# Two transformer blocks on one core: the norms' gains in rows, held weight splits, and a new order in the mixers

## The chip, the cores and the metric

The kernel runs on one core of a Trainium2 chip. The core has five engines that run their own instruction lists in order and meet at semaphores: TensorE (PE, matmuls into PSUM), VectorE (DVE), ScalarE (ACT), GpSimd (POOL) and SyncE (SP, which here issues most DMAs). The metric is the time of one execution in microseconds (us); lower is better.

## What is computed

256 tokens of width 1024 in float32 go through two blocks.

```
h = layer_norm(x, ln_in)                                   # block 1
for l in 0, 1:
    mix = mixer(h)      # MLA, differential and forgetting attention, one w_in, one w_out
    h   = layer_norm(alpha * h + mix, ln1[l])
    ffn = grouped_moe(h)   # router: 16 experts in 4 groups, top 2; silu(h wg) * (h wu) @ wd
    h   = layer_norm(alpha * h + ffn, ln2[l])
mem_k, mem_v = split(rms_norm(mem) @ mem_wkv)              # block 2
for i in 0, 1:
    x += 0.5 * swiglu(rms_norm(x), ffn1[i])
    x += ssd_pool_mixer(rms_norm(x)) if i == 0 else swa_sink_attention(rms_norm(x))
    x += memory_cross_attention(rms_norm(x), mem_k, mem_v)
    x += 0.5 * swiglu(rms_norm(x), ffn2[i])
```

The MLA part has 8 heads, the differential and the forgetting parts 4 each; the forgetting part adds cumulated log-sigmoid decays to its scores. The window attention has 16 heads, 4 key heads, a window of 128, a linear bias per head and one sink per head; the cross attention has 4 heads of width 256 over 256 memory rows.

## The kernel before

The tokens are two tiles of 128 rows (`t` = 0, 1). A product that must be exact to float32 is three matmuls on split numbers, `mm3` (L483 to L485): each operand is a high part `h` and a rest `l`, and hi·hi, hi·lo and lo·hi are summed in PSUM. `split` (L488, L489) makes the two from an activation: a copy on ScalarE, a subtraction on VectorE. The experts' and the memory's weights are used as plain float32 and aren't split.

All weights come through the class `Stream` (L66): a list of 1 MB transfers on SP's queue, into rings of 7 "stage" and 6 "piece" tiles, in the order of a plan (`plan`, L331). A weight to be split is read from its stage tile: a copy on ScalarE (L161) and a subtraction on VectorE (L162) into a piece tile. `hold(key)` stops these splits before a key, `go()` lets them run on. A raw expert tile is used where it lands, and may land in a buffer of the activations that is free (a slot: `m1`, `m4`, `xl`, `xh`). A framework's scheduler sets the order on each engine from the program's order, the dependences, and `with self.after(...)`, which puts instructions behind given ones.

Block 1's mixer (`mixer`, L818) takes w_in in six column blocks, runs MLA's heads between blocks 2 and 3, and the other two attentions behind the last. Its parts named below: the copies of the memory's keys on VectorE (L1729), the rotation tables (L744), the copies of MLA's values on ScalarE (L966), the softplus of the forget gates with its table load (L655, in `fox_decay`, L1071). A norm (`LayerNorm`, L194) is done tile by tile as the sums of a layer come in: `ln_norm` (L570) leaves out gain and bias, which are then applied in columns on the transposed rows (L548, L550, or at the experts' gather L1319, L1320, with the router's weights multiplied by them once) and later in rows (`gain`, L601 and L602); `ln_full` (L592 to L596) applies them at once with two passes over a tile.

The experts (`moe`, L1208) go in pairs, `pr` = 0 to 7: gate and up (L1352), transposes (L1369), down (L1386), and a scatter (L1401) whose results VectorE adds to the residual (L1403). Four gathers (L1317) fetch the tokens' columns. Memory products (L1758) fill TensorE beside the router and behind the last scatter.

In block 2 the SSD mixer's heads run four at a time (L2166, L2175) with the products for z (L1623 to L1625, copied out at L2189) in between; the window attention (`swa`) computes keys and values, both halves of the queries, and then the heads pair by pair: scores (L1980, L1982), bias and maximum (L2000), softmax, transposes and values; the cross attention (`xattn`) computes queries (L1831), scores and values between two products, `xq` and `xo`.

## Time and profile before

| | us |
|---|---|
| median of 3 runs | 2002.53 |
| lowest, highest | 2001.2, 2002.54 |
| profiled execution | 2002.3 |
| its span | 2000.5 |
| TensorE busy in the span | 1935.0 (97%) |
| VectorE, ScalarE busy | 1127.0, 866.9 |
| mean granted clock | 0.986 of full |

The page of a profile gives busy times, then the span in forty slices with the granted clock of TensorE in tenths. A view of waits sums, for each line, how long the engine stood idle just before it and which instruction released it. A timeline lists instructions by start; a bracket at the end of a row is the idle time before it and its releaser. A view of windows gives busy time, granted clock and the DMA engines' share for stretches of time.

### The profile page before, as it was taken

To read this page: it belongs to the slowest core of one execution; us is meant where nothing else is said; L and a number is where in the kernel's file an instruction comes from. 1 tells how busy PE (TensorE), PEld (TensorE's weight loads), DVE (VectorE), ACT (ScalarE), POOL (GpSimd) and SP (SyncE) were. 2 spreads that over 40 slices of the span, in tenths; PEclk is the share of its full clock that TensorE was granted. 3 is DMA by queue.
4 is the path that set the end of the run, shared out by engine and by line. 5 is a ranking of instruction groups with operands and counts; after the bars stand their busy time and mean duration, and the time that the engine had idled before them with its cause. 6 is when DMAs were issued, how large, how long until landed. Compare 5 with 4: busy or idle time off the path is not lost.

```text
span 2000.5 us, 28009 instructions
## 1 busy us (share of the span) xinstructions
PE 1935.0 (97%) x11069; PEld 1458.6 (73%) x11069; DVE 1127.0 (56%) x2211; ACT 866.9 (43%) x1539; POOL 58.0 (3%) x119
## 2 busy tenths in 40 slices
PE   6999999999999998899999899999999999999999
PEld 6776433367864333599988887899989986778998
DVE  7775122167751221656579775655665567766554
ACT  6563110136631101455466555644454455556443
POOL 1110000000100000000001000000000000000000
PEclk9999999999999999999999999999999997999999
DMA  8456999973569999855564353455555543335550
GB/s 290 145 203 229 397 419 420 421 256 123 206 236 403 420 421 421 300 187 181 186 202 137 132 219 109 163 190 190 190 200 186 182 165 137 127 99 175 190 190 22
DMA packets 176044, 453.39 MB, mean 227 GB/s; under 512 B 11120, under 2 KB 106844, under 8 KB 149148
## 3 DMA queue, kind: packets, MB, share of 16 engines
q1 hardware_dynamic: 172044, 435.55, 59.1%
q0 software_dynamic: 3856, 15.91, 2.2%
q8 instruction: 91, 1.49, 0.3%
q14 instruction: 53, 0.43, 0.1%
HBM read 446.19 MB, written 5.24 MB: 226 GB/s over the span
## 4 chain that ended last, share of the span: by engine, by line
PE 56%; DMA 5%; DVE 3%; ACT 2%; issue 0%; POOL 0%; DVEq 0%; SPq 0%; POOLq 0%; ACTq 0%
PE mm L1623 7%; PE mm L1625 7%; PE mm L1624 7%; PE accb L485 5%; PE accb L484 5%; PE accb L483 4%; PE acca L485 4%; PE acca L484 4%; PE acca L483 4%; DMA piece<-in_exp_w_gate_dram 2%; DMA piece<-in_exp_w_down_dram 1%; DMA stage<-in_exp_w_down_dram 1%; DMA stage<-in_exp_w_up_dram 1%; DVE piece L162 1%; PE mm L1876 1%; PE mm L541 1%
## 5 line engine op out<-in xcount | busy, mean ns | idle before, releaser
L162 DVE TENSOR_TENSOR piece<-stage,piece 128x1024 fp32r<-128x1024 f32 (+3 forms) x439 | 513.8, 1179 | 240.9 <-ACT piece L161 239.3
L161 ACT ACTIVATE piece<-stage 128x1024 fp32r<-128x1024 f32 (+3 forms) x439 | 444.5, 1021 | 343.8 <-PE mm L1625 204.4
L1352 PE MATMUL mm<-stage,m 128*64 128x512 f32 x512 | 221.8, 595 | 0.0
L1352 PE MATMUL mm<-piece,m 128*64 128x512 f32 x480 | 215.1, 596 | 2.0 <-DMA piece<-in_exp_w_up_dram 2.0
L1623 PE MATMUL mm<-m,piece 128*128 128x256 f32 x736 | 207.0, 281 | 2.3 <-DVE m L2189 2.3
L1624 PE MATMUL mm<-m,piece 128*128 128x256 f32 x736 | 206.7, 281 | 0.0
L1625 PE MATMUL mm<-m,piece 128*128 128x256 f32 x736 | 206.6, 281 | 0.0
L1623 PE MATMUL mm<-xh,piece 128*128 128x256 f32 x576 | 163.1, 283 | 0.0
L1625 PE MATMUL mm<-xh,piece 128*128 128x256 f32 x576 | 163.0, 283 | 0.0
L1624 PE MATMUL mm<-xl,piece 128*128 128x256 f32 x576 | 162.9, 283 | 0.0
L484 PE MATMUL accb<-piece,m 128*128 128x512 f32 (+1 forms) x364 | 144.3, 397 | 0.0
L485 PE MATMUL accb<-piece,m 128*128 128x512 f32 (+1 forms) x364 | 143.7, 395 | 0.5 <-DVE m L493 0.5
L483 PE MATMUL accb<-piece,m 128*128 128x512 f32 (+1 forms) x364 | 143.1, 394 | 0.9 <-ACT m L950 0.7
L1623 PEld LDWEIGHTS mm<-m,piece 128*128 128x128 f32 x736 | 139.4, 189 | 4.6 <-issue 3.0
L1624 PEld LDWEIGHTS mm<-m,piece 128*128 128x128 f32 x736 | 139.3, 189 | 1.9 <-issue 0.3
L1625 PEld LDWEIGHTS mm<-m,piece 128*128 128x128 f32 x736 | 139.4, 189 | 0.0
L483 PE MATMUL acca<-piece,m 128*128 128x512 f32 (+1 forms) x348 | 138.2, 398 | 0.2
L485 PE MATMUL acca<-piece,m 128*128 128x512 f32 (+1 forms) x348 | 137.2, 396 | 0.5 <-DVE m L493 0.5
L484 PE MATMUL acca<-piece,m 128*128 128x512 f32 (+1 forms) x348 | 137.7, 396 | 0.0
L1352 PEld LDWEIGHTS mm<-stage,m 128*64 128x64 f32 x512 | 65.1, 137 | 76.4 <-issue 73.8
L1623 PEld LDWEIGHTS mm<-xh,piece 128*128 128x128 f32 x576 | 110.4, 192 | 1.3
L1624 PEld LDWEIGHTS mm<-xl,piece 128*128 128x128 f32 x576 | 110.4, 192 | 1.2
(567 smaller groups left out, 3535.8 us busy)
## 6 DMA issues: line engine op xcount, KB each, us to landing
stage<-in_ffn_wi_dram SPq DMA_DIRECT2D x88, 1024.0 KB, 5.5
stage<-in_ffn_wo_dram SPq DMA_DIRECT2D x44, 1024.0 KB, 5.4
stage<-in_exp_w_down_dram SPq DMA_DIRECT2D x38, 1024.0 KB, 18.6
stage<-in_exp_w_up_dram SPq DMA_DIRECT2D x34, 1024.0 KB, 11.2
stage<-in_exp_w_gate_dram SPq DMA_DIRECT2D x30, 1024.0 KB, 18.5
piece<-in_exp_w_gate_dram SPq DMA_DIRECT2D x30, 1024.0 KB, 17.9
piece<-in_exp_w_up_dram SPq DMA_DIRECT2D x30, 1024.0 KB, 15.0
piece<-in_exp_w_down_dram SPq DMA_DIRECT2D x26, 1024.0 KB, 16.8
```

The lines of the kernel that those rows point to most:

```text
L161: nc.scalar.activation(wh, src, AF.Copy)
L162: nc.vector.tensor_tensor(wl, src, wh.bitcast(F32), op=OP.subtract)
L483: nc.tensor.matmul(out, ah, bh, start=first, stop=False)
L484: nc.tensor.matmul(out, ah, bl, start=False, stop=False)
L485: return nc.tensor.matmul(out, al, bh, start=False, stop=last)
L541: self.moved = nc.tensor.transpose(p[:, k * P:(k + 1) * P], src[:, 4 * q + k:D:8], self.c["ident"])
L1352: mm = nc.tensor.matmul(o[64 * k:64 * k + 64, :], x[:, j, s:s + CAP], w[k][:, jj, :], start=(j == 0), stop=(j == 7))
L1623: nc.tensor.matmul(out, wh[:, j, :], hi[:, j, :], start=(j == 0), stop=False)
L1624: nc.tensor.matmul(out, wh[:, j, :], lo[:, j, :], start=False, stop=False)
L1625: nc.tensor.matmul(out, wl[:, j, :], hi[:, j, :], start=False, stop=(j == 7))
L1876: nc.tensor.matmul(po[:, k * P:(k + 1) * P], v[:, mc, h * 256 + cc * P:h * 256 + (cc + 1) * P], pt[t][:, (2 * h + mc) * P:(2 * h + mc + 1) ...
```

## The change

It has seven parts.

1. Every norm of block 1 is `ln_full` with gain and bias in rows, loaded as rows of `gv` tiles. The columns, `gain` and the router's folded weights go; the gather copies plainly.
2. The norm behind a mixer splits its two tiles for the gather only behind tile 1's last pass; the first norm's weight splits are held behind its transposed splits.
3. In the stream four expert tiles, not two, land in activation buffers, two gathers move by a pair or two, the second memory weights come before the next layer's first weights, and the first of the next layer's held splits run behind the next norm's copies.
4. `fox_decay` stands behind MLA's heads; one rotation moves from GpSimd to VectorE.
5. The window attention does query half 0, keys and values, the first four head pairs, query half 1, the other four.
6. In the cross attention the last query tile is done bank by bank, its transposes come behind the last query matmul, and the output weights' splits are held until the last probabilities.
7. In the SSD mixer four kinds of copies out of PSUM go from VectorE to ScalarE.

The diff, cut to its core:

```diff
 class LayerNorm:
     def tile(self, t):
-        self.sqrt, self.last = k.ln_norm(self.res, t)
+        self.sqrt, self.last = k.ln_full(self.res, t, self.gb)
         if self.plain:
...
+            with k.after(self.sqrt, self.last):
+                for i in range(2):
+                    v = self.res[:, i, :].rearrange("p (f j) -> p j f", j=8)
+                    k.split(v, self.hh[:, i], self.hl[:, i])
...
-    def gain(self, gb=None):
-        for t in range(2):
-            self.k.ln_gain(self.res, t, gb or self.gb)
...
+            slots = {("up", 0, 4): "m4", ("down", 0, 0): "xl", ("down", 1, 0): "m1", ("down", 0, 4): "xh"}
...
+                    if n == NSTAGE + NPIECE - 2:
+                        early("down", 1, 0)
+                        early("down", 0, 4)
+            mem(1024 * l + 512)
...
+                gb = self.load_gb(I["ln_in_g"], I["ln_in_b"], eng=nc.sync)
                 self.load_ident()
-                self.gain_columns(0)
+                self.ws.start(1)
...
+        self.ws.limit = 0
+        ln = LayerNorm(self, res, gb, ("xh", "xl"))
         ln.tile(0)
...
+            if l == 0 and bi == 0:
+                with self.after(*norm.half):
+                    ws.go(2)
+                with self.after(norm.last, norm.sqrt):
+                    ws.go()
...
-            with self.after(at[1]):
-                norm.gain()
...
         block(2)
-        self.fox_decay(ff, fb, qkf)
...
+        self.fox_decay(ff, fb, qkf)
         qkd = self.m(5)[:, :2048].rearrange("p (k t h d) -> p k t h d", k=2, t=2, h=8)
...
-            self.rope(qkd[:, k, :, :, 0:8], 4, 8, self.cos_d, self.sin_d, nc.gpsimd)
+            self.rope(qkd[:, k, :, :, 0:8], 4, 8, self.cos_d, self.sin_d, nc.vector)
...
-                nc.scalar.activation(x[:, j0, :], p[:, 0:256], AF.Identity, scale=g1[:, j0:j0 + 1], bias=b1[:, j0:j0 + 1])
-                at = nc.vector.tensor_scalar(x[:, j0 + 1, :], p[:, 256:512], g1[:, j0 + 1:j0 + 2], b1[:, j0 + 1:j0 + 2],
-                                             op0=OP.mult, op1=OP.add)
+                nc.scalar.activation(x[:, j0, :], p[:, 0:256], AF.Copy)
+                nc.vector.tensor_copy(x[:, j0 + 1, :], p[:, 256:512])
...
-                if pr == 8:
-                    with self.after(state["silu"], state["tr"]):
-                        ws.go(4)
...
             with self.after(at):
                 nxt.tile(0)
+            with self.after(*nxt.copied):
+                ws.go(2)
...
-        self.gemm_rows("xq", 8, lambda k: (hi[:, k, :], lo[:, k, :]), acc=rows(), done=queries, cuts=(2,))
+        ws.hold("xo")
+        self.gemm_rows("xq", 8, lambda k: (hi[:, k, :], lo[:, k, :]), acc=rows(), done=chain, cuts=(2,), by_bank=True)
+        with self.after(self.last_mm):
+            for x in steps:
+                next(x, None)
...
+        with self.after(at[3]):
+            ws.go()
...
-        queries(0, 1)
+        attend(0, bias, "xl")
         queries(1, 1)
-        attend(0, bias, "xl")
...
-            nc.vector.tensor_tensor(zs[:, ch, :], p[:, 0:256], rrow, op=OP.mult)
+            nc.scalar.activation(zs[:, ch, :], p[:, 0:256], AF.Copy)
+            nc.vector.tensor_tensor(zs[:, ch, :], zs[:, ch, :], rrow, op=OP.mult)
```

How this stands on the engines, at three places. First ScalarE's order in layer 0's mixer before, from the copies of MLA's queries (L950) to the copies of its transposed queries and keys (L975); `gv` are the value copies, `sp_e` the softplus.

```order
46 L161 ACTIVATE piece<-stage 128x1024
47 L161 ACTIVATE piece<-stage 128x512 x2
48 L655 ACT_TABLE_LOAD
49 L655 ACTIVATE sp_e<-sp_a 128x8
50 L966 ACTIVATE gv<-accb 128x256 x2
51 L966 ACTIVATE gv<-acca 128x256 x2
52 L975 ACTIVATE m_750<-mm 98x4x128
```

And now:

```order
41 L163 ACTIVATE piece<-stage 128x512
42 L946 ACTIVATE gv<-accb 128x256 x2
43 L163 ACTIVATE piece<-stage 128x512
44 L946 ACTIVATE gv<-acca 128x256 x2
45 L631 ACT_TABLE_LOAD
46 L631 ACTIVATE sp_e<-sp_a 128x8
47 L955 ACTIVATE m_686<-mm 98x4x128
```

The table load and the softplus moved from before the value copies to behind them.

Second VectorE's order at layer 0's norm behind the mixer, tile 1. `res` is the residual, `m_1639` the rest part of the split for the gather, `xh` the transposed rows for the router.

```order
292 L489 TENSOR_TENSOR m_1639<-res,m_1638 128x1024
293 L565 COPY xh<-mm 128x4x128
294 L578 BN_STATS bnst<-res 128x6 x2
295 L579 BN_AGGR bnmv<-bnst 128x2
296 L527 TENSOR_SCALAR sq_v<-bnmv 128x1
297 L528 RECIPROCAL sq_t<-sq_t 128x1
298 L529 TENSOR_SCALAR sq_y<-sq_t,sq_v 128x1
299 L530 TENSOR_SCALAR sq_y<-sq_y 128x1
300 L531 TENSOR_TENSOR lnr<-sq_y,sq_t 128x1
301 L581 TENSOR_SCALAR res<-res,bnmv,lnr 128x1024
302 L489 TENSOR_TENSOR m_1639<-res,m_1638 128x1024
303 L565 COPY xh<-mm 128x4x128
```

And now:

```order
297 L561 COPY xh<-mm 128x4x128
298 L574 BN_STATS bnst<-res 128x6
299 L575 BN_AGGR bnmv<-bnst 128x2
300 L576 SCALAR_TENSOR_TENSOR res<-res,bnmv,gv 128x1024
301 L528 TENSOR_SCALAR sq_v<-bnmv 128x1
302 L529 RECIPROCAL sq_t<-sq_t 128x1
303 L530 TENSOR_SCALAR sq_y<-sq_t,sq_v 128x1
304 L531 TENSOR_SCALAR sq_y<-sq_y 128x1
305 L532 TENSOR_TENSOR lnr<-sq_y,sq_t 128x1
306 L578 SCALAR_TENSOR_TENSOR res<-res,lnr,gv 128x1024
307 L490 TENSOR_TENSOR m_1666<-res,m_1665 128x1024 x2
308 L561 COPY xh<-mm 128x4x128
```

Tile 0's split moved from before tile 1's statistics to behind tile 1's norm, so two splits now stand in front of the last copy for the router.

Third TensorE's order at the start of the window attention before: the last query product (L483 to L485), the first scores (L1980, L1982), transposes of query half 1 (L1967).

```order
7366 L483 MATMUL accb<-piece,m_16266 128x512
7367 L484 MATMUL accb<-piece,m_16266 128x512
7368 L485 MATMUL accb<-piece,m_16267 128x512
7369 L1980 MATMUL acca<-m_16394,m_16392 128x128 x2
7370 L1982 MATMUL acca<-m_16394,m_16392 128x256 x2
7371 L1980 MATMUL acca<-m_16394,m_16392 128x128 x2
7372 L1982 MATMUL acca<-m_16394,m_16392 128x256
7373 L1967 MATMUL mm<-ident,xh 128x128 x8
```

And now, with query half 1's product still running (L483 to L485) and scores on L1958, L1960:

```order
7356 L1958 MATMUL acca<-m_16335,m_16333 128x128 x2
7357 L1960 MATMUL acca<-m_16335,m_16333 128x256 x2
7358 L483 MATMUL accb<-piece,m_16207 128x512
7359 L484 MATMUL accb<-piece,m_16207 128x512
7360 L1958 MATMUL acca<-m_16335,m_16333 128x128
7361 L1960 MATMUL acca<-m_16335,m_16333 128x256
7362 L1958 MATMUL acca<-m_16335,m_16333 128x128
7363 L1960 MATMUL acca<-m_16335,m_16333 128x256
7364 L485 MATMUL accb<-piece,m_16208 128x512
7365 L483 MATMUL accb<-piece,m_16207 128x512
```

The first scores moved from behind query half 1's product to between its last matmuls, 18 of 48 of which are left behind them.

## Rows read from the trace of the kernel before

**Rows 1.** The page: span, TensorE's busy time, its granted clock.

```profile
span 2000.5 us, 28009 instructions
...
PE 1935.0 (97%) x11069; PEld 1458.6 (73%) x11069; DVE 1127.0 (56%) x2211; ACT 866.9 (43%) x1539; POOL 58.0 (3%) x119
...
PEclk9999999999999999999999999999999997999999
```

**Rows 2.** Waits of TensorE: line, releaser, total, times, longest.

```profile
PE accb L483 <- ACT xh L488: 4.7, 1, 4.7
...
PE acca L1980 <- DVE wnm L2000: 4.5, 2, 4.2
...
PE mm L541 <- DVE sq_y L530: 4.0, 1, 4.0
...
PE mm L1401 <- DVE res L1403: 4.0, 7, 1.8
...
PE tp L2175 <- DVE prob L2166: 3.4, 2, 2.3
...
PE mm L1837 <- DVE m L1831: 3.2, 2, 1.6
...
PE accb L483 <- ACT gv L966: 2.5, 1, 2.5
...
PE mm L1623 <- DVE m L2189: 2.3, 1, 2.3
...
PE mm L1724 <- DVE m L1729: 2.2, 1, 2.2
...
PE mm L1352 <- DMA piece<-in_exp_w_up_dram: 2.0, 2, 1.3
...
PE accb L1386 <- DMA stage<-in_exp_w_down_dram: 2.1, 2, 1.3
...
PE mm L916 <- DVE rope_w L744: 1.6, 1, 1.6
```

**Rows 3.** Timelines of VectorE, first norm and a full norm: start, duration.

```profile
6.26 0.84 DVE L581 TENSOR_SCALAR res<-res,bnmv,lnr 128x1024 f32<-128x1024 f32 x1
...
416.97 1.27 DVE L594 SCALAR_TENSOR_TENSOR res<-res,bnmv,gv 128x1024 f32<-128x1024 f32 x1
```

**Rows 4.** Groups by line, 36 to 43 us, VectorE: busy, mean ns.

```profile
L601 DVE TENSOR_TENSOR res<-res,gv 128x1024 f32<-128x1024 f32 x2 | 2.4, 1217 | 0.0
```

**Rows 5.** Windows: length, busy PE, PEld, DVE, ACT, POOL, clock, DMA share, GB/s.

```profile
44.00:46.00 2.00, 1.07 (x4) 0.67 (x4) 1.67 (x12) 0.99 (x4) 0.28 (x3) 0.62 1.09 352
...
50.00:52.00 2.00, 2.00 (x10) 1.90 (x9) 2.00 (x13) 1.98 (x4) 0.74 (x1) 0.68 0.30 123
```

**Rows 6.** Timeline of ScalarE, 62 to 66 us.

```profile
63.62 1.28 ACT L655 ACT_TABLE_LOAD   x1
```

**Rows 7.** Timelines around the router of layer 0, three engines.

```profile
163.51 2.08 ACT L488 ACTIVATE m<-res 128x1024 fp32r<-128x1024 f32 x1 [0.25 <-DVE res L581]
...
167.56 0.69 DVE L565 COPY xh<-mm 128x512 f32<-128x512 f32 x1
...
172.76 0.29 PE L1269 MATMUL tp<-gsel,blob 128*128 128x16 f32 x2
```

**Rows 8.** Windows, layer 0's expert loop.

```profile
350.00:400.00 50.00, 46.21 (x193) 15.97 (x190) 9.29 (x14) 5.07 (x8) 0.28 (x3) 1.00 1.01 421
```

**Rows 9.** Timeline of VectorE at layer 0's last scatter.

```profile
410.38 1.81 DVE L162 TENSOR_TENSOR piece<-stage,piece 128x768 fp32r<-128x768 f32 x2
```

**Rows 10.** Windows of 10 us in the window attention.

```profile
1690.00:1700.00 10.00, 10.00 (x33) 5.96 (x32) 4.21 (x24) 5.00 (x20) 0.00 (x0) 0.50 0.00 0
```

**Rows 11.** Timeline of VectorE there: the first score row of every other head pair.

```profile
1685.78 0.29 DVE L2000 CUSTOM_DVE_ANT_0 prob<-acca,m 128x128 f32<-128x128 f32 x1 [1.29 <-PE mm L1150]
...
1702.37 0.29 DVE L2000 CUSTOM_DVE_ANT_0 prob<-acca,m 128x128 f32<-128x128 f32 x1 [3.55 <-PE mm L1150]
...
1712.72 0.29 DVE L2000 CUSTOM_DVE_ANT_0 prob<-acca,m 128x128 f32<-128x128 f32 x1 [0.64 <-PE mm L1150]
```

More of the change, by code (lines that the diff above doesn't have):

```diff
@@ L103, in raw @@
     def raw(self, key, ap, a, b, ring=0, slot=None):
-        self.units.append(dict(ap=ap, a=a, b=b, left=1, tile=None, ring=ring, slot=slot, first=len(self.pieces)))
+        first = max((p["n"] + 1 for p in self.pieces if not p.get("raw")), default=0)
+        self.units.append(dict(ap=ap, a=a, b=b, left=1, tile=None, ring=ring, slot=slot, first=first))
         u = len(self.units) - 1
@@ L112, in use @@
         self.pieces.append(dict(key=key, u=u, raw=True, n=len(self.pieces)))
+        return self.pieces[-1]
     def _room(self, ring):
@@ L484, in mm3 @@
         nc.tensor.matmul(out, ah, bl, start=False, stop=False)
-        return nc.tensor.matmul(out, al, bh, start=False, stop=last)
+        self.last_mm = nc.tensor.matmul(out, al, bh, start=False, stop=last)
+        return self.last_mm
     def split(self, src, hi, lo):
@@ L816, in block1, with mixer @@
         return res, ln
-    def mixer(self, l, norm, res, steps=None, moe=None):
+    def mixer(self, l, norm, res, steps=None):
         nc, I, c, ws = self.nc, self.I, self.c, self.ws
@@ L1210, in moe @@
         n, hh, hl = ln.n, ln.hh, ln.hl
-        x = self.slot("m1")
-        rows = [x[:, 0:D], x[:, D:2 * D]]
-        for r, v in zip(rows, (I["ln1_g"], I["ln1_b"])):
-            nc.gpsimd.dma_start(r, bcast_rows(v, D, l * D))
+        ws.free.append("m1")
         sc = self.sm(32, "gsc")
@@ L1318, in gather @@
                         nc.tensor.matmul(o, hl[:, t, j, :], m, start=False, stop=(t == 1))
-                nc.scalar.activation(x[:, j0, :], p[:, 0:256], AF.Identity, scale=g1[:, j0:j0 + 1], bias=b1[:, j0:j0 + 1])
-                at = nc.vector.tensor_scalar(x[:, j0 + 1, :], p[:, 256:512], g1[:, j0 + 1:j0 + 2], b1[:, j0 + 1:j0 + 2],
-                                             op0=OP.mult, op1=OP.add)
-            return at
-        at = gather(0)
-        with self.after(at):
-            ln.gain(rows)
+                nc.scalar.activation(x[:, j0, :], p[:, 0:256], AF.Copy)
+                nc.vector.tensor_copy(x[:, j0 + 1, :], p[:, 256:512])
+        gather(0)
         self.memory_gemm(l, 0, [self.prob()[:, 0:512] for t in range(2)], {7: [at_pp]})
@@ L1357, in gate_or_up @@
                 ws.release(2)
+            state["last"] = mm
             return o
@@ L1441, in moe @@
                 y = down(pr - 1, at)
+            if pr == 1:
+                gather(1)
             if pr < 8:
@@ L1842, in queries, with chain @@
                          nc.vector.tensor_scalar(qv[:, :, 1, :], pv[:, :, 1, :], g[:, 1:2], None, op0=OP.mult))
[L1843 to L1847 removed]
+            for b in banks:
+                s = self.acc(t)
+                sc.setdefault(t, []).append(s)
+                for h in range(2):
+                    for cc in range(2):
+                        nc.tensor.matmul(s[:, h * 256:h * 256 + 256], qT[:, 4 * b + 2 * h + cc, ts[t]],
+                                         kT[:, 4 * b + 2 * h + cc, :], start=(cc == 0), stop=(cc == 1))
+        normed, steps = [], []
+        def chain(*x):
+            steps.append(queries(*x))
+            next(steps[-1])
         def attend(t):
```

268 lines of the change are left out of this document (109 added, 159 removed).

## The prediction

> **What bounds the kernel now.** I read the page first: TensorE is busy 1935.0 of the 2000.5 us of the span and its clock is full in all but one of forty slices [rows 1]. So 65 us of idle time, and what the half clock adds to busy time, is all that a change of order can win; a stage is worth what TensorE waits in it. The profiled execution took 2002.3 us, 1.8 us more than the span, and stands 0.2 us below the median of 2002.53; what is taken off the span comes off the median.
>
> Next the waits of TensorE [rows 2]: they are few, each a few us long, and most name VectorE or ScalarE. Then the 2 us windows around such a wait, to see whether the clock falls: of the four windows from 44 to 52 us the first was granted 0.62 and the last 0.68 [rows 5], the two between 0.50, after TensorE had idled for 2.2 us on L1729 and before it idled 1.6 on L744. The busy time in these windows (1.07, 0.99, 2.00, 2.00 us) at those clocks gives 0.41 + 0.50 + 1.00 + 0.64 = 2.6 us lost. So 3.8 us of waiting cost 6.4 here. Last the timelines of single places, for the price of each operation.
>
> **The change, part by part** (plus is time won).
>
> *First norm.* The pass that ends it, 0.84 us on a tile, becomes two of 1.27 [rows 3], so tile 0's rows are ready 2 x 1.27 - 0.84 = 1.7 us later. In return the gain operations in columns, eight on each of VectorE and ScalarE for the two tiles, leave the way to the first split, and the first weights' splits go behind the copies: part of the 4.7 us wait on xh [rows 2] goes. The last two of the first block's weight splits now wait for tile 1's last pass, which I set at 1 us. Bounds: -2.5 (1.7 and 0.8 of late splits, nothing back) and +2 (nearly half of the 4.7 goes); I take -0.8, nearer the passes that have a row.
>
> *Gains out of layer 0's mixer.* Four products of 1.22 us (the group has two of them, the line below it the others) stood on VectorE behind the first block [rows 4], 4.9 us in front of the copies that L1729 and L744 wait for. They go entirely, so the 3.8 us of waits and the 2.6 of half clock go with them unless the splits beside them are late next. Bounds 2 and 6.4; I take 5.5.
>
> *Forget decay later.* ScalarE loads a table for 1.28 us [rows 6] ahead of the copies of MLA's values, and TensorE waits 2.5 us for them [rows 2]. Now the copies come first, as the piece of ScalarE's order in the section on the change shows, and more matmuls of the uq/ukv products stand ahead of the transposes. The 2.5 go, and by the ratio of the place above (2.6 lost for 3.8 waited) 1.7 of half clock. The load stays in the row, now ahead of the copies of the transposed queries, so some of it may be the next wait. Bounds 0 and 4.2; I take 3.0, a little above the bare wait. The twelve rotation operations that move from GpSimd to VectorE lie in a stretch with no wait of TensorE; I cost them at nothing, and at a fourth of a 1.22 us product's width, 0.3 each and 3.7 in all, if the cover by block 4's matmuls were gone [rows 4]. (The Trainium skill, "ScalarE: Activation LUTs", section "What ACT_TABLE_LOAD costs", puts a load at about 2.7 us; the trace has 1.28. By the page's figure the load would stick out 1.4 us more, this term would be 1.6 and the whole sum below 22.9; the trace decides.)
>
> *Norm behind the mixer, twice.* Before, tile 1's split on ScalarE begins at 163.51, right behind the norm, and the last copy of the transposed rows ends at 167.56 + 0.69 = 168.25, 4.7 us later; TensorE gets the ranks at 172.76 without a gap [rows 7]. Now both tiles' splits stand ahead of that last copy. On ScalarE: 2.08, a table load of 1.28 and its warming 0.2, 2.08; then VectorE's second split, 2.0, and the copy, 0.69: 8.3 us after the norm, 3.6 later than before. The norm itself ends about 1 us earlier, since tile 0's split no longer lies in front of tile 1's statistics (-2.06) and only one more pass does (+1.27). So the router comes 2.5 us later, the four memory matmuls that cover the ranks are the same number, and TensorE waits it out: -2.5 a layer, -5.0. Bounds 0 (the norm ends earlier by more) and -9 (3.6 each and half clock behind). The 4.9 us of gains that stood behind the router lay beside a busy TensorE and win nothing.
>
> *Expert stream.* In the loop the transfers run at 421 GB/s, share 1.01 [rows 8]: the queue is saturated, 1 MB in 2.49 us. The waits on expert weights, 2.0 and 2.1 us [rows 2], are the whole loss (two of 1.0 stand lower in the same view and aren't counted). The new plan puts four tiles rather than two into freed buffers, 2 x 2.49 = 5 us of lead, and its first ring tile is freed earlier. I take +4.1; bounds 0 (the buffers come free too late to matter) and +6.
>
> *Held splits at the ends of the layers.* In layer 0 two groups of two splits, 1.81 us each [rows 9], lay ahead of the last scatter's additions on VectorE: 3.6 us won. They come back behind the norm's copies, where one group is uncovered: -1.8. In layer 1 the 4.0 us wait on the norm [rows 2] goes, and two splits behind the gain copies cost about 2: together +3.9. Bounds -4 (both held groups uncovered) and +9 (nothing comes back, and the half clock behind the waits goes).
>
> *SSD.* Copies go from VectorE to ScalarE. The waits are 3.4 on L2166 (longest 2.3) and 2.3 on L2189 [rows 2]. The latter is a bank that VectorE empties late; the former came with the last two head groups back to back, and now 32 of the z matmuls lie between these. 2.3 + 2.3 = +4.6. Bounds 1 and 8, the upper with all of the 5.7 and the half clock behind it.
>
> *Cross attention, twice.* The wait on the queries is 1.6 each, 3.2 in all [rows 2]; the chain of the last tile's first bank now runs beside its second bank. But the output weights' splits are held until the last probabilities. +2.0; bounds -3 and +3.2.
>
> *Window attention.* TensorE waits 4.5 us [rows 2] and then runs at 0.50 [rows 10]: two head pairs take 1702.37 - 1685.78 = 16.6 us at the low level, 1.2 GHz, and 1712.72 - 1702.37 = 10.4 at the high one [rows 11]. The first two pairs run low as well, for some 2.5 us of loss. If all of it goes: 4.5 + 6.2 + 2.5 = 13.2. But only 18 of the 48 matmuls of query half 1 are left for the first half's pairs, and in the second half's first two pairs just eight large matmuls are left as filler, against 15 before the third: there the low clock can return at the 6.2 of two pairs. +7.0; bounds 0 and 13.2.
>
> Sum: -0.8 + 5.5 + 3.0 - 5.0 + 4.1 + 3.9 + 4.6 + 2.0 + 7.0 = 24.3 us; 2002.3 - 24.3 = 1978.0.
>
> **Rivals.**
> 1. *The window attention wins nothing.* A head pair is a chain through VectorE and ScalarE of 5.2 us at the high clock; query half 1's own chain is now pushed into it, and the low clock moves to the second half. For it: the filler counts above. Against: VectorE was busy 4.2 of 10 us in the low stretch [rows 10]. 1978 + 7 = 1985.
> 2. *Every wait goes with its half clock.* 6.4 + 4.2 + 6 + 9 + 7 + 3.2 + 13.2 less 0.8 and 5 = 43: 1959. For it: these are distinct places with the cause removed at each. Against: each place has a next-latest engine within a few us.
> 3. *The held and moved splits cost at every place.* Start -2.5, norms -9, ends -4, cross attention -3, the rest as forecast (5.5 + 3 + 4.1 + 4.6 + 7 = 24.2): 5.7 won, 1996.6. For it: in-order engines, and one split per engine takes about 1 us. Against: a gemm uses four pieces one after the other, only the first can stall.
> 4. *Slower: the clock falls behind the late router.* In the window attention a wait of 4.5 us was followed by a long low stretch: of four 10 us windows the middle two had 0.50 (the second of them is in [rows 10]), those beside them 0.80 and 0.83, in all 27 us at the low level and 13.5 lost. If the 3.6 us behind each router does that to the gather and the first experts, it costs 3.6 + 13.5 a layer, 34.2, in place of the 5.0: 1978.0 + 29.2 = 2007.2. It decides from 22 us of low clock a layer on: 2 x (3.6 + 11) is the 24.3 and the 5.0 already in it. Against: the wider matmuls that follow are dense, and the dip behind two waits in the mixer was over in 8 us [rows 5].
>
> **How the numbers follow.** The forecast, 1970 to 1984, 0.42; rival 1, 0.20; rival 2, 0.15; rival 3, 0.13; rival 4, 0.07; 0.03 for the stream's slots and splits coming out without effect, near 1990. A measurement here tells about 0.2%, 4 us, from no change. Faster by more: the forecast, rivals 1 and 2, the last case, and a half of rival 3: 0.86. Same: the rest of rival 3, 0.06. Slower: rival 4, and a little for costs not seen, 0.08. The range reaches to rival 2 below and rival 3 above: 1959 to 1997.
>
> **What would show it.** TensorE's waits of the profile after should have no L1729, L744 and L966 in them, nor waits on expert weights; a new wait of 2 to 3 us should stand before the rank matmuls or the gather, once a layer. The gap before the second pair of scores in the window attention should be gone and its low clock shorter than 15 us. The forecast is wrong if low clock stands for more than 10 us in the expert loop, if TensorE's idle time is still above 55 us, or if its busy time grew.

## The result, and the profile after

The changed kernel takes 1956.54 us (median of four runs, 1955.89 to 1957.53), the kernel before 2002.53 beside it (2001.2 to 2002.89): the ratio is 0.9772, 95% interval 0.9755 to 0.9789. The forecast was 1978.0, its range 1959 to 1997; the sign was right, the size 21.5 us short, and the result lies 2.5 us below the range.

The page of the kernel after, the lines that answer to [rows 1]:

```profile
span 1954.0 us, 27935 instructions
...
PE 1909.8 (98%) x11029; PEld 1445.2 (74%) x11029; DVE 1118.3 (57%) x2226; ACT 862.7 (44%) x1550; POOL 46.6 (2%) x93
...
PEclk9999999999999999999999999999999999999999
```

The span is 46.5 us shorter. TensorE's idle time (span less busy) falls from 65.5 to 44.2; what the half clock adds to busy time (from windows of 2 us over the whole span, busy time by one less the granted clock) falls from 23.8 to 4.8. That is 21.3 and 19.0. Of the last 6.2, some 2 are the forty small matmuls of the router's folded weights, which the kernel after no longer has (11069 and 11029 on the two pages). In the rest, matmuls run closer together at the full clock; no listed wait names it.

TensorE's waits after, against [rows 2]:

```profile
PE mm L542 <- DMA ident<-consts_dram: 13.0, 1, 13.0
PE mm L1129 <- DVE prob L1994: 3.7, 2, 3.1
PE mm L542 <- DVE sq_y L531: 2.6, 2, 1.3
...
PE accb L1810 <- ACT m L1803: 1.8, 2, 0.9
...
PE accb L483 <- ACT piece L163: 1.4, 1, 1.4
...
PE mm L1362 <- DVE res L1364: 1.3, 4, 0.3
...
PE acca L1810 <- ACT m L1803: 1.1, 2, 0.5
```

The waits on the memory's keys, the rotation tables and MLA's values are gone or down to 0.3 or less; those on the expert weights, on the SSD heads and on z are gone. The wait on the norm at a layer's end (L541 before, L542 now, on sq_y) was one of 4.0 and is two of 1.3; the scatter's longest wait fell from 1.8 to 0.3. New are the first row, where TensorE's first instruction stands behind the identity, and the second, in the window attention. By stretches of the program, each from the first matmul of a kind to the first of the next:

| stretch (us) | before | after | won | forecast |
|---|---|---|---|---|
| start to first weight product | 13.9 | 16.3 | -2.5 | -0.8 |
| layer 0's mixer | 143.7 | 134.2 | 9.5 | 8.5 |
| router, both layers | 34.3 | 35.1 | -0.9 | -5.0 |
| gather to the next norm's transposes, layer 0 | 247.3 | 234.8 | 12.5 | } 8.0 |
| the same, layer 1 | 247.6 | 236.7 | 11.0 | } |
| layer 1's mixer, first SwiGLU | 332.1 | 331.2 | 0.9 | 0 |
| SSD mixer | 112.8 | 106.0 | 6.9 | 4.6 |
| cross attention, two | 136.8 | 132.8 | 3.9 | 2.0 |
| window attention | 105.0 | 98.9 | 6.2 | 7.0 |
| the other SwiGLUs and outputs | 627.1 | 628.1 | -1.0 | 0 |

The sum is 46.5, against 24.3 forecast. Of the 22 us that were missed, 15.4 lie in the two expert loops and the ends of the layers.

### The profile page after: what moved, and what is told of

The parts are those of the page before. It is cut to its first block, busy times and chain, and to the rows that moved or that the text cites. A ratio compares the mean times of both kernels' runs of the same rounds, so it can differ in the third digit from the quotient of the medians.

```text
span 1954.0 us, 27935 instructions
## 1 busy us (share of the span) xinstructions
PE 1909.8 (98%) x11029; PEld 1445.2 (74%) x11029; DVE 1118.3 (57%) x2226; ACT 862.7 (44%) x1550; POOL 46.6 (2%) x93
## 4 chain that ended last, share of the span: by engine, by line
PE 61%; ACT 3%; DVE 2%; issue 0%; ACTq 0%; DVEq 0%
PE mm L1583 8%; PE mm L1584 8%; PE mm L1582 8%; PE accb L483 4%; PE acca L485 4%; PE accb L485 4%; PE accb L484 4%; PE acca L484 4%; PE acca L483 4%; PE mm L1312 3%; PE accb L1347 1%; PE acca L1347 1%; ACT piece L163 1%; PE mm L1846 1%; DVE piece L164 1%; PE mm L542 1%
## 5 line engine op out<-in xcount | busy, mean ns | idle before, releaser
L1312 PE MATMUL mm<-stage,m 128*64 128x512 f32 x528 | 231.7, 600 | 0.0
L483 PE MATMUL accb<-piece,m 128*128 128x512 f32 (+1 forms) x364 | 143.7, 395 | 1.0 <-ACT m L493 0.9
L485 PE MATMUL accb<-piece,m 128*128 128x512 f32 (+1 forms) x364 | 143.6, 395 | 0.5 <-DVE m L494 0.5
L485 PE MATMUL acca<-piece,m 128*128 128x512 f32 (+1 forms) x348 | 137.6, 396 | 0.8 <-DVE m L494 0.8
L483 PE MATMUL acca<-piece,m 128*128 128x512 f32 (+1 forms) x348 | 137.9, 397 | 0.2
## 6 DMA issues: line engine op xcount, KB each, us to landing
stage<-in_exp_w_down_dram SPq DMA_DIRECT2D x34, 1024.0 KB, 12.9
stage<-in_exp_w_up_dram SPq DMA_DIRECT2D x32, 1024.0 KB, 11.3
piece<-in_exp_w_down_dram SPq DMA_DIRECT2D x24, 1024.0 KB, 14.9
```

What stands on the lines that cost most here:

```text
L483: nc.tensor.matmul(out, ah, bh, start=first, stop=False)
L485: self.last_mm = nc.tensor.matmul(out, al, bh, start=False, stop=last)
L1312: mm = nc.tensor.matmul(o[64 * k:64 * k + 64, :], x[:, j, s:s + CAP], w[k][:, jj, :], start=(j == 0), stop=(j == 7))
```

## The experiments

Each ran once, with a profile, beside the kernel before (1999.5 to 2005.1 in these groups). That spread hides a few us, so a verdict rests on stretches of the trace, which repeat better: layer 1's mixer, where no edit touched it, takes 135.9 to 136.2 in seven versions of the kernel after. What the half clock adds to a stretch is worked out from windows as above; it comes and goes between kernels, so it is given beside the stretch.

### What the expert stream, its slots and the gathers are worth

The theory at first was that the loops won by lead, that is by more tiles that land early in freed buffers. The rival was that the gathers' place and the release of splits won.

Kernel after, two slots and the old rule for the ring:

```diff
-            slots = {("up", 0, 4): "m4", ("down", 0, 0): "xl", ("down", 1, 0): "m1", ("down", 0, 4): "xh"}
+            slots = {("up", 0, 4): "m4", ("down", 0, 0): "xl"}
-        first = max((p["n"] + 1 for p in self.pieces if not p.get("raw")), default=0)
+        ... first=len(self.pieces)
```

> The changed kernel with the expert stream nearly as before: two expert tiles in activation buffers rather than four, and the old rule for when a raw tile may enter the second ring. Stretch from the first gather to the next norm's first transposes: 247.3 and 247.7 us before, 234.8 and 236.7 in the changed kernel. Theory 1 (the weights come earlier, and with them go waits and small stretchings of matmuls that no row shows): 7 to 10 us longer in each layer, 1971 to 1977 in all. Theory 2 (VectorE and ScalarE are relieved of gains, column copies and early splits, the lead of the stream does little): under 1.5 us a layer, 1957 to 1960.

Measured: 1959.0. Gather to transposes takes 237.4 and 237.4 (after 234.8, 236.7); 1.7 of this in layer 0 is half clock that the kernel after hasn't. No wait on expert weights came back. Lead alone is worth about 1 us a layer.

Kernel after with the two slots alone:

> The changed kernel with only two of its four expert tiles in activation buffers (m4 and xl; the other two go through the rings), the rule for the second ring as changed. Theory 1: two tiles of 2.49 us less lead, so 3 to 6 us longer in each layer, 1963 to 1968. Theory 2: 0 to 1 us, 1957 to 1959.

Measured: 1961.92; 239.1 and 237.8, of which 3.4 each are half clock (the kernel after has 3.4 in layer 1 alone), so again about 1 us a layer. One wait on expert weights came back, 0.5.

Kernel before with one more slot, `xh`, for ("down", 0, 4):

> The kernel before with one expert tile more (the second half of expert 0's down weights) in the buffer xh, free behind the router. Theory 1: one tile of 2.49 us more lead takes 2 to 3 us off each layer, 1996 to 1999. Theory 2: no change, 2001 to 2003.

Measured: 1999.78; 244.6 and 246.7, 2.7 and 0.9 less than before. Layer 1 has 1.7 of half clock that the kernel before hasn't; without it 2.6. There a tile of lead is worth the 2 to 3 us a layer of theory 1.

Kernel before with gathers 1 to 3 at their later places:

```diff
-            if pr == 2:
-                gather(2)
-            if pr == 4:
-                gather(3)
+            if pr in (3, 5):
+                gather(pr // 2 + 1)
```

> The kernel before with only the three later gathers moved as in the change (gather 1 behind the first down product, 2 and 3 one pair later). First gather to the second memory product: 239.0 and 236.5 us before, 227.4 and 225.7 in the changed kernel with its old stream and without a clock dip. Theory G (TensorE frees ring tiles earlier when the gathers, 3.8 us each, don't stand in front of the first experts, so the saturated stream runs ahead): most of the 10 us a layer, 5 to 10 each, 1983 to 1992. Theory V (VectorE's gains and column copies made the loop longer): under 1.5 us each, 1999 to 2003.

Measured: 1993.62; gather to the memory product 236.4 and 234.9 (before 239.0, 236.5): 2.5 and 1.6 less, between the two theories. Without any new slot the waits on expert weights fall from 6.3, all rows together, to 2.4:

```profile
PE acca L1386 <- DMA piece<-in_exp_w_down_dram: 2.0, 2, 1.3
...
PE mm L1352 <- DMA piece<-in_exp_w_up_dram: 0.4, 1, 0.4
```

Its other gain is not the edit's: the window attention, untouched, took 57.0 us from its scores on instead of 63.4 (below).

Kernel after with stream, slots, gathers and the selection's transposes as before:

> The changed kernel with the stream, its two slots (both for gate tiles), and the places of the gathers and of the transposed selection all as before; norms in rows, plain copies and held splits as changed. Theory G: the loops are again 236 to 238 us, 10 us a layer more than the changed kernel, 1974 to 1979. Theory V: 228 to 230 us, 1959 to 1963.

Measured: 1964.32; 237.8 and 242.8, together 9.1 more than after (10.8 more without the half clock, which is 1.7 here and 3.4 after). Of the waits on expert weights 5.5 are back, the longest row first:

```profile
PE accb L1343 <- DMA stage<-in_exp_w_down_dram: 2.5, 2, 1.3
```

So these are worth more together than one by one, as far as it was tried: the gathers alone were moved in the kernel before only.

### The held splits: an interaction

Kernel after, four held splits released at the last pair, as before, and not two behind the norm's copies:

```diff
+                if pr == 8:
+                    with self.after(state["silu"], state["tr"]):
+                        ws.go(4)
-            with self.after(*nxt.copied):
-                ws.go(2)
```

> The changed kernel with the next layer's first four weight splits released at the last pair again, as before, in place of two behind tile 0's copies and the rest behind tile 1's. If the splits in front of the last scatter were what cost 3.6 and 4.0 us at the layers' ends: 3 to 5 us longer at each end, 1962 to 1967. If the ends were won by weights that come earlier: under 1 us each, 1956 to 1959.

Measured: 1967.76. Up to the memory product the loops stay as they are; from there to the transposes it takes 11.8 and 12.9 us, not 8.4, with waits on the norm of 4.8 and 5.9, and the mixer behind takes 138.2, not 136.0.

Then the same edit put alone into the kernel before:

> The kernel before with only the change's release of the next layer's weight splits: two behind tile 0's copies and the rest behind tile 1's, in place of four at the last expert pair. Undoing this in the changed kernel cost 11 us. First gather to the next norm's first transposes: 247.3 and 247.7 us before. If the held splits are worth what undoing them cost: 4 to 6 us a layer, 1991 to 1995. If they are worth the 2 us a layer of the prediction's term, and the 11 us came from the changed kernel's other order: 1997 to 2000.

Measured: 2006.98, 5.8 slower than the kernel before beside it: from the memory product 10.9 and 11.3, the mixer 139.8. What wins when it is there loses when it comes alone. VectorE's order there suggested why: three splits ran between the last additions and the norm although they were held. `Stream._split` splits everything that stands ahead in the list when a weight is taken, and in the kernel before the second memory weights stand behind the next layer's first weights. The theory is that release and list order work only together; the rival that some other part of the kernel before spoils the release. Four kernels tell them apart, with this line of the plan moved:

```diff
+            mem(1024 * l + 512)
             if l == 0:
                 ...
                 self.plan_block("w_in", ...)
-            mem(1024 * l + 512)
```

> The kernel before, with one line of the plan moved: the second memory weights stand before the next layer's first weights in the list of transfers. The release of held splits is as before. Theory 1 (order and release work only together): gather to memory product 238 to 240 us in layer 0, 236 to 238 in layer 1 (before 239.0, 236.5), memory product to the next norm's transposes 8 to 11.5, the mixer behind 136.5; in all within 1.5 us of before. Theory 2 (the order of the list is a cause by itself, since memory weights no longer wait for the next layer's): the loop and its end shorter by 3 us or more in each layer.

> The kernel before with both: held splits released two behind the norm's copies, the rest later, and the second memory weights before the next layer's first weights in the list. Theory 1 (together they work): memory product to transposes 8.0 to 8.8 in both layers (b_hold 10.9, 11.3), mixer behind 136 to 137 (b_hold 139.8), gather to memory product 234 to 236.5 in each layer; shorter than before by 5 to 10 us in these stretches. Theory 2 (the order of the list does nothing; b_hold was slow by something else of the kernel before): 10.5 to 11.5, 139 to 140, as b_hold.

> The kernel after with that line moved back: the second memory weights behind the next layer's first weights. Theory 1: taking a memory weight forces the held splits ahead of it in the list, as in b_hold: memory product to transposes 10 to 11.5 (after 8.4), the mixer behind it 138 to 140 (after 136.0), 1963 to 1970 in all. Theory 2 (no effect): 8.4, 136.0, 1956 to 1960.

> The kernel before with release, order of the list, and gathers 1 to 3 at their later places. If the parts add up: gather to memory product 231.5 to 234.5 in layer 0 and 231.5 to 234.5 in layer 1 (after 226.4 and 224.9 less its dip of 3.4), transposes 8 to 8.8 behind, so 11 to 14 us of the 23.5 won in the two loops and ends, and the rest is the stream's slots. If order and gathers are one cause (both only take the waits on transfers away): no shorter than 235.

Measured, with both layers' stretch from gather to transposes, and the stretch behind it (layer 1's mixer and the first SwiGLU):

| kernel | time | loops and ends | behind | sum | half clock in it | without |
|---|---|---|---|---|---|---|
| before | 2002.53 | 494.9 | 332.1 | 826.9 | 4.9 | 822.0 |
| + release | 2006.98 | 498.1 | 335.7 | 833.8 | 9.9 | 823.9 |
| + list order | 2004.81 | 498.0 | 335.5 | 833.5 | 9.8 | 823.7 |
| + both | 1999.24 | 490.0 | 332.1 | 822.1 | 5.1 | 817.0 |
| + both + gathers | 1988.8 | 484.5 | 332.1 | 816.6 | 3.4 | 813.2 |
| after | 1956.54 | 471.4 | 331.2 | 802.6 | 3.4 | 799.2 |
| after - release | 1967.76 | 480.0 | 334.1 | 814.0 | 7.7 | 806.3 |
| after - list order | 1970.99 | 484.3 | 333.3 | 817.6 | 12.0 | 805.6 |

Each half alone costs 6.6 to 6.9 us, both together win 4.9: what the pair does beyond its halves is 18.3. More than half of that is half clock. Without it each half alone costs 1.7 to 1.9, both win 5.1, and the pair does 8.7 beyond its halves. Taken from the kernel after, the halves cost 11.4 and 15.0, without the half clock 7.1 and 6.4. So the interaction holds by either count, and its size does not. At the waits of the layers' ends the five kernels without the pair have 3.2 to 4.7 of half clock and the three with it none; the rest lies mostly behind the gathers, which the pair doesn't touch. By its whole time list order alone stood level with the kernel before beside it (2004.81 and 2005.08), because its window attention came out in the short form told below.

The theory had list order alone at nothing, and that fell; the rival fell on all four. The gathers add 5.5 to the pair, alone they won 3.6; without the half clock it is 3.8 both times. VectorE's timelines show the mechanism at layer 0's end; first the kernel after without the list order, columns as in [rows 3]:

```profile
396.02 2.56 DVE L1363 SCALAR_TENSOR_TENSOR res<-res,mm 128x512 f32<-128x512 f32 x4
398.50 2.69 DVE L164 TENSOR_TENSOR piece<-stage,piece 128x768 fp32r<-128x768 f32 x3
401.11 1.87 DVE L573 BATCH_NORM_STATS2 bnst<-res 128x6 f32<-128x512 f32 x3
```

and the kernel after:

```profile
393.23 2.63 DVE L1364 SCALAR_TENSOR_TENSOR res<-res,mm 128x512 f32<-128x512 f32 x4
395.77 1.87 DVE L574 BATCH_NORM_STATS2 bnst<-res 128x6 f32<-128x512 f32 x3
...
404.32 1.28 DVE L490 TENSOR_TENSOR xl<-mm,xh 128x512 fp32r<-128x512 f32 x2
405.53 1.83 DVE L164 TENSOR_TENSOR piece<-stage,piece 128x768 fp32r<-128x768 f32 x2
```

In the first, 2.69 us of splits lie between the additions and the statistics; in the second the statistics follow at once and the splits stand behind the norm's copies. With the list order but the old release (b_mem, the kernel before with that line moved) all four stand between the norm's passes:

```profile
414.05 1.27 DVE L595 SCALAR_TENSOR_TENSOR res<-res,bnmv,gv 128x1024 f32<-128x1024 f32 x1
415.23 3.55 DVE L162 TENSOR_TENSOR piece<-stage,piece 128x768 fp32r<-128x768 f32 x4
```

TensorE's wait for the norm in the kernel after without the list order, layer 0's and layer 1's:

```profile
PE mm L541 <- DVE sq_y L530: 3.9, 1, 3.9
...
PE mm L541 <- DVE res L577: 5.9, 1, 5.9
```

With the list order of the change, these are the two of 1.3 in the waits after.

Last, the kernel after with all of this undone at once: stream, slots, gathers, list order, release.

> The kernel after with all that concerns the expert loop and the layer ends as before: the stream's plan and rule, two slots, the gathers' places, the place of the second memory weights, and the release of held splits. Norms, mixers and the parts of block 2 stay as after. Gather to the next norm's transposes, both layers in all, without the clock's dips: before 490.5, after 468.1, with stream, slots and gathers alone undone 478.8. If these parts explain the whole gain: 489 to 492. If only release and order of the list add their 5.6 (as in the kernel before): 484 to 485, and some 6 us of the gain belong to the gains that no longer stand beside the router and the gather.

Measured: 1974.0; 490.2 and 332.5, in all 822.7, of which 7.9 are half clock. So of the 24.3 us won in these stretches (826.9 to 802.6), 20.1 belong to these parts: 9.1 to stream, slots and gathers (811.7 with them undone), 10.9 to release and list order. Without the half clock the parts win 15.6 of 22.9: 10.8 and 4.7. The other 7.3 stay with the rest of the change. Of these 1.7 are work that only moved: two memory matmuls a layer, 0.43 each, stand ahead of the gather now and count to the router. No run names the last 5.6. The kernel after has no gains in columns; whether that is the cause stays open.

### The norm behind the mixer

Kernel after, each tile's split at once:

```diff
-            with k.after(self.sqrt, self.last):
-                for i in range(2):
-                    v = self.res[:, i, :].rearrange("p (f j) -> p j f", j=8)
-                    k.split(v, self.hh[:, i], self.hl[:, i])
+            v = self.res[:, t, :].rearrange("p (f j) -> p j f", j=8)
+            self.parts = k.split(v, self.hh[:, t], self.hl[:, t])
```

> The kernel after with the splits for the gather as before, tile 0's at once behind its own norm; the norm stays in rows. First router transposes to gather: before 17.1 in each layer, after 17.6. If a split in front of the last copy costs the router 2.5 us, as the forecast had it: 15.0 to 15.5. If ScalarE's split already lies beside tile 1's norm, as the trace after has it: 17.3 to 18.5, the early split now in front of tile 1's statistics costing up to 1 us, and no gain.

Measured: 1958.29; the router takes 20.2 us in each layer, not 17.6. Both expectations were short: the old place costs 2.6 a layer there. Two more memory matmuls come ahead of the gather with it, and the loops get shorter; router and loop together, without the half clock, cost 1.5 and 1.3. The kernel after, ScalarE and VectorE, against [rows 7]:

```profile
153.36 2.06 ACT L489 ACTIVATE m<-res 128x1024 fp32r<-128x1024 f32 x1
155.44 1.28 ACT L505 ACT_TABLE_LOAD   x1
156.74 0.20 ACT L505 ACTIVATE warm<-eps 128x1 f32<-128x1 f32 x1
156.85 2.05 ACT L489 ACTIVATE m<-res 128x1024 fp32r<-128x1024 f32 x1
...
155.31 1.28 DVE L578 SCALAR_TENSOR_TENSOR res<-res,lnr,gv 128x1024 f32<-128x1024 f32 x1
156.51 2.01 DVE L490 TENSOR_TENSOR m<-res,m 128x1024 fp32r<-128x1024 f32 x1
158.93 2.01 DVE L490 TENSOR_TENSOR m<-res,m 128x1024 fp32r<-128x1024 f32 x1 [0.41 <-ACT m L489]
160.86 0.68 DVE L561 COPY xh<-mm 128x512 f32<-128x512 f32 x1
```

and with each split at once:

```profile
151.43 2.01 DVE L486 TENSOR_TENSOR m<-res,m 128x1024 fp32r<-128x1024 f32 x1 [1.07 <-ACT m L485]
153.35 0.68 DVE L557 COPY xh<-mm 128x512 f32<-128x512 f32 x1
153.95 1.28 DVE L570 BATCH_NORM_STATS2 bnst<-res 128x6 f32<-128x512 f32 x2
...
163.03 0.69 DVE L557 COPY xh<-mm 128x512 f32<-128x512 f32 x1
```

In the kernel after, tile 0's copy on ScalarE runs at 153.36 to 155.42, while VectorE still norms tile 1 (to 156.59); the last copy for the router ends 4.95 us behind the norm (before 4.74). With the split at once, VectorE's 1.07 of waiting and 2.01 of split lie ahead of tile 1's statistics.

### The gains that left

Kernel before without the gains of layer 0's mixer (`norm.gain()` left out, so the residual stays without them):

> The kernel before without the four products of gain and bias behind the mixer's first block (the residual is then left without the first norm's gain and bias, so the output differs). Prediction's term: the waits on L1729 and L744 and their half clock go, 5.5 us of the stretch from the first product to the norm behind the mixer (143.7 us), 1995 to 1998. Rival: the copies of the memory's keys are late anyway behind the splits, under 2 us, 2000 to 2002.

Measured: 1998.42; the mixer takes 141.0, not 143.7. The waits on L1729 and L744, 3.8 together, fall to 0.6, and this one comes, with 2.6 us of half clock around it:

```profile
PE accb L483 <- ACT m L948: 3.8, 1, 3.8
```

Alone the removal wins 2.7, not the forecast 5.5. The new wait goes back to a transfer: GpSimd clears the buffer of MLA's queries only when the copy of the memory's transposed rows out of it (`memT`) has landed, ScalarE's copies wait for GpSimd, and TensorE for these. The copy took 7.2 us here, 4.3 in the kernel before. The mixer's 9.5 needs the rest too.

Kernel before without the gains in rows behind the router:

> The kernel before without the four products of gain and bias in rows behind the first gather of each layer (the residual is then left without ln1's gain and bias, so the output differs). Theory V: 4.9 us of VectorE gone, 3 to 5 us off each layer's loop, 1993 to 1997. Theory G: under 1 us each, 2000.5 to 2003.

Measured: 2001.05, loops and ends 246.9 and 248.5 (before 247.3 and 247.6): 4.9 us of VectorE behind the router cost nothing, as the forecast had it.

### The SSD copies

Kernel before with the four kinds of copies out of PSUM on ScalarE:

```diff
-            nc.vector.tensor_tensor(zs[:, ch, :], p[:, 0:256], rrow, op=OP.mult)
+            nc.scalar.activation(zs[:, ch, :], p[:, 0:256], AF.Copy)
+            nc.vector.tensor_tensor(zs[:, ch, :], zs[:, ch, :], rrow, op=OP.mult)
```

> The kernel before with only the SSD mixer's copies on ScalarE. From the heads' first product to the pool product: 41.2 us before, 35.6 in the changed kernel. If the copies' engine and the order that follows from it are all: 35 to 36 us and 7 us in all with the 1.4 before the heads, 1994 to 1997. If part came from the phase of the clock dips: 37 to 39 us, 1997 to 2000.

Measured: 1989.99. The SSD mixer takes 70.4 and 35.6 us to and from its heads (before 71.6, 41.2; after 70.4, 35.6), and from 1085 to 1135 us, around its heads, no wait of TensorE is listed any more: its 6.9 us are shown to be these copies. The window attention is again in its short form, 57.0 from the scores on, which is not the edit's.

### The start

Two tries to get the first norm's 2.5 us back in the kernel after. The identity first, the gain rows on ScalarE's queue:

> The changed kernel with the identity loaded ahead of the first norm's gain and bias rows, and these on ScalarE's DMA queue in place of SyncE's. In the changed kernel the first norm waits 3.9 us for the gain row and TensorE starts at 13.0, behind the identity. If the rows were late because they stood behind others in one queue: first matmul product 2 to 4 us earlier and 2 to 4 us in all, 1953 to 1955. If the rows are slow by themselves: under 1 us, 1956 to 1957.

Measured: 1964.16, worse: VectorE got the second half of tile 0 itself only at 9.15, the first weight product stood at 17.0, and a new wait of 6.2 us appeared in the mixer (140.7, not 134.2).

The rows loaded once as 4 KB and spread by GpSimd:

> The changed kernel with the first norm's gain and bias loaded as one row each (4 KB) and spread over the partitions by GpSimd, in place of two transfers of 512 KB; a broadcast takes 1.3 us. If the start is bound by the bytes in front of the identity and the first weights: TensorE starts at 8 to 9 us rather than 13.0, the first product comes at 13 to 14 rather than 16.3, 1953 to 1955. If the first weights' arrival sets the first product whatever the norm does: 1956 to 1958.

Measured: 1962.68: TensorE starts at 11.5, the first product stands at 14.9, but the mixer took 138.9, with a wait of 5.1 us on ScalarE. In both the wait is the one of the gains above: ScalarE stands behind GpSimd, and GpSimd behind the `memT` copy. GpSimd in the kernel after and in the first try:

```profile
53.42 0.13 POOL L907 MEMSET m<- 128x32 f32 x1 [4.01 <-DMA memT<-m]
```

```profile
59.16 0.13 POOL L907 MEMSET m<- 128x32 f32 x1 [9.01 <-DMA memT<-m]
```

The copy took 4.5 us after, 9.4 and 9.0 in the two tries. In both a 1 MB weight transfer was issued 0.5 us ahead of it, where in the kernel after it comes 1.6 us behind. That this is why it took longer was not tried. No version that I ran beats the kernel after.

## Why the prediction was right or wrong

*What bounds it.* Right: what was won is idle time (21.3) and half clock (19.0) of TensorE and 6.2 of busy time, and the clock is full in all forty slices.

*Expert stream and held splits, 4.1 + 3.9.* This is where it failed: 23.4 measured. The step is the price of the stream. "The waits on expert weights ... are the whole loss" took two rows, 4.1 us, and put the rest of TensorE's idle time in the loops at nothing. Windows from the gather to the second memory product, both layers, before:

```profile
174.69:413.67 238.98, 229.08 (x1049) 94.03 (x1049) 61.42 (x98) 32.20 (x53) 5.28 (x14) 0.99 0.95 384
575.55:812.01 236.46, 226.80 (x1047) 94.46 (x1047) 58.84 (x92) 32.90 (x53) 5.12 (x7) 1.00 0.95 387
```

and after:

```profile
168.08:394.52 226.44, 223.48 (x1047) 92.59 (x1047) 50.87 (x89) 26.57 (x49) 5.25 (x14) 1.00 0.98 400
556.43:784.73 228.30, 225.31 (x1046) 93.49 (x1046) 50.45 (x86) 26.57 (x49) 5.06 (x7) 0.99 0.96 398
```

TensorE idled 9.9 and 9.7 us there and idles 3.0 and 3.0 now. Waits on expert weights were 6.3 of the 19.6; others stood on the additions to the residual, on the experts' activations and on the memory's own weights. With stream, slots and gathers undone the idle time is 12.6, and the loops take 9.1 us more. In the kernel after the queue is as full as in [rows 8]:

```profile
320.00:370.00 50.00, 49.36 (x216) 17.46 (x214) 10.79 (x16) 5.07 (x8) 0.00 (x0) 1.00 1.01 427
```

TensorE is busy 49.4 of 50 us there, for 46.2 before, at nearly the same rate of the queue. For the held splits I counted "3.6 us won" and "-1.8" back in layer 0, as if the edit were one. It is two that need each other, the place in the list and the release. Both together win 4.9 in the kernel before, near the 3.9, but that is luck: the release that I priced loses 6.9 there by itself. In the kernel after the two are worth 10.9, 4.7 without the half clock. I read the plan's line as a matter of the stream's order and did not ask which splits a taken weight forces.

*Norm behind the mixer, -5.0.* Wrong by 4.1: -0.9. "Now both tiles' splits stand ahead of that last copy. On ScalarE: 2.08, a table load ..." put both of ScalarE's splits behind the norm. The first ran beside it, so the last copy ends 4.95 us behind the norm and not 8.3. And the memory matmuls ahead of the gather are not "the same number": two more (0.86 us) stand there and cover the ranks, so nothing waits, and 1.7 of the stretches' loss is work that left the loops.

*Layer 0's mixer, 5.5 + 3.0.* The sum was about right (9.5). How it divides was not shown: the removal of the gains alone gives 2.7 and uncovers the wait behind the `memT` copy, and the later forget decay was not run by itself. The wait on MLA's values went from 2.5 to 0.3. Of the 1.4 us more that the prediction weighed for a table load nothing shows: in ScalarE's rows above the load takes 1.28, and the instructions on both its sides stand 0.02 us from it.

*First norm, -0.8.* Measured -2.5; seven kernels with the same start have their first product at 14.8 to 15.7, so -0.9 to -1.9 there. The wait of 4.7 did shrink, to 1.4. The cause of the loss is one I did not price, the landing of the gain row, and 0.4 of the identity (the norm's last pass ends at 12.5):

```profile
9.14 1.29 DVE L576 SCALAR_TENSOR_TENSOR res<-res,bnmv,gv 128x1024 f32<-128x1024 f32 x1 [3.91 <-DMA gv<-in_ln_in_g_dram]
...
12.96 1.94 PE L542 MATMUL mm<-ident,res 128*128 128x128 f32 x8 [12.96 <-DMA ident<-consts_dram]
...
16.32 0.69 PE L483 MATMUL accb<-piece,xh 128*128 128x384 f32 x1 [1.42 <-ACT piece L163]
```

*SSD, +4.6.* The mechanism was right and the size short, 6.9: the half clock behind the waits (2.3 us by the windows from 1112 to 1120) went too, which I had kept for the upper bound.

*Cross attention, +2.0.* 3.9, over the upper bound of 3.2: the wait on the queries, 1.6 each, became smaller ones, which is 2.0 less idle time in the two, and no wait on the held output weights is listed. The other 1.9 are shorter busy time that no row names.

*Window attention, +7.0.* 6.2 measured, and the nearness is luck: rival 1, that it wins nothing, is nearer to the mechanism. Ten kernels have the old order. Three, the kernel before among them, take 62.7 to 63.5 us from the scores on, seven 57.0 to 57.1, and the code there is the same. The three lost 10.9 to 13.0 us to the half clock there, the seven 5.5. Where [rows 10] has 0.50, the kernel before with later gathers has the full clock; behind it stands the new order's own low window:

```profile
1690.00:1700.00 10.00, 10.00 (x59) 6.48 (x59) 7.28 (x38) 5.72 (x23) 0.00 (x0) 1.00 0.00 1
```

```profile
1650.00:1660.00 10.00, 7.30 (x37) 5.05 (x37) 7.56 (x27) 6.89 (x17) 0.00 (x0) 0.83 0.31 107
```

All ten kernels with the new order take 59.4 to 60.7 there and 39.4 to 39.6 before the scores (41.6 in the old), in all 98.8 to 100.1. The old order in its short form takes 98.6 to 98.7. So the new order wins nothing over the short form and 6 over the long one. The new order's wait of 3.7 (L1129) is nearly the 4.5 that went. What it does is to keep out the long form. Why the old order takes one form or the other was not tried.

*Rivals.* Rival 2, that every wait goes with its half clock, 1959 with 0.15, came closest: 19 of the 46 us are half clock. Rivals 3 and 4 did not come: 3.4 us lost to the half clock behind one router at most, and of rival 3's costs the start's -2.5 alone, by another cause. Of the signs I named, the waits went and the half clock in the window attention became short; the new wait before the ranks or the gather did not appear. My signs of error said low clock over 10 us in the loop, idle time over 55, more busy time; none occurred, and none could have told of a gain that was forecast too small.

## What to carry to other kernels

Before the waits that an edit takes away are priced, set them beside all the idle time of the bottleneck engine in that stretch: what the listed rows leave over needs a reason too. When an edit releases held work at another place, ask what forces that work earlier: a list that is served in order may force it whatever the release says, and then the release alone does harm. Try an edit of an order in both kernels, alone and left out, before a price is given to it. Where a stretch has a low clock, look whether the same code has it in other versions of the kernel before its cure is counted as a gain.

## What the runs showed of the hardware that I had not expected

In these runs the half clock came or stayed away with the code unchanged: behind the two-column matmuls that follow the gather (32 in 4.46 us, no wait of TensorE near them) the same code lost 0, 1.7 or 3.4 us in different kernels. Layer 1 of the kernel after, the timeline of TensorE and then the windows:

```profile
562.09 4.46 PE L1293 MATMUL tp<-ggate,gv 128*128 128x2 f32 x32
566.47 1.11 PE L1312 MATMUL mm<-stage,m 128*64 128x512 f32 x1
...
571.58 0.59 PE L1312 MATMUL mm<-stage,m 128*64 128x512 f32 x1
```

```profile
566.00:568.00 2.00, 2.00 (x7) 0.98 (x9) 0.33 (x2) 0.00 (x0) 0.00 (x0) 0.50 0.98 360
568.00:570.00 2.00, 2.00 (x8) 0.52 (x6) 0.00 (x0) 0.00 (x0) 0.00 (x0) 0.50 0.29 111
```

A row spread over 128 partitions by its transfer, issued at 1.66 us as the third on the queue, was there at 9.14; the identity behind two such rows at 12.96. One copy of the memory's rows, 1 MB on GpSimd's queue, took 4.3 to 9.4 us in different kernels, and with it moved a wait of TensorE of up to 6.2.
